# Two layers of a network on one core: the long-lived tiles 2080 bytes apart instead of 2048, the parts of the weights 4128 instead of 4096

## The chip, the cores and the metric

The kernel runs on one core of one Trainium2 chip. The metric is the device time of one execution in microseconds. Three runs of the kernel before took 2134.65, 2132.99 and 2131.47 us; the median is 2132.99 us. A core has five instruction streams: TensorE (PE; its weight loads are listed apart as PEld), VectorE (DVE), ScalarE (ACT), GpSimd (POOL) and SyncE (SP, which here issues DMAs). They run beside each other and meet at semaphores.

## What is computed

The input is one sequence of 512 tokens with 1024 features, and everything is float32. Three blocks follow one another.

1. A mixed block: RMS norm, one wide projection `h @ w_in`, sparse attention over 8 heads (a compressed branch, a selected branch and a window branch, gated), retention over 4 heads, two output projections gated and summed, `w_out`, then an MLP `square(relu(h @ w_up)) @ w_down` with 4096 hidden features.
2. An mLSTM layer (8 heads, a stabilised matrix memory) with a convolutional feed-forward of 2816 hidden features behind it: `h @ w_up`, a causal convolution of width 3 along the tokens, a GELU gate, `@ w_down`.
3. A forgetting-attention layer (16 heads) on keys and values that are projected once, and the same kind of feed-forward.

Most of the arithmetic is in products of 512 tokens with weight matrices of 1024 to 5632 columns:

```
h = rmsnorm(x, norm);  proj = h @ w_in;  ...;  x = x + mixer(proj) @ w_out
h = rmsnorm(x, norm);  x = x + act(h @ w_up) @ w_down
```

## The kernel before, in words

**Where tiles lie.** On-chip memory has 128 partitions, and a tile of shape [128, 512] in float32 takes 2048 bytes of each. Such a tile is called a unit here. Units come from one pool by tag: tag "u" has 48 buffers for what lives long (the activations' two halves, the residual stream, queries, keys, values, outputs of projections), "P" has 8, "PT" 12 and "e" 5 for short-lived ones (line 25). The buffers of a tag lie one behind the other, so that those of "u" start 2048 bytes apart. The function `unit` (line 210) picks tag and buffers. Raw weights land in two tiles of 8192 bytes (`raw`, line 150). Their two parts lie in four buffers `wh` and four `wl` of 1024 columns, 4096 bytes each (lines 167 and 168). As the program is laid out, every unit and every part begins at one remainder of its address modulo 512 bytes, which is 480; a slice of 128 columns is 512 bytes, so that nearly every operand of a large product begins there too. This remainder is called the phase below.

**How a product is made.** Float32 precision comes from three products of rounded operands. A weight block is split by ScalarE into a rounded part `wh` (line 169) and by VectorE, for a few chunks by GpSimd, into the rest `wl = raw - wh` (line 171). An activation tile is split in the same way into `hi` and `lo` (`split`, from line 369). Then `mm3` (lines 474 to 478) multiplies `hi` by `wh`, `lo` by `wh` and `hi` by `wl` into one accumulator. The weight is the stationary operand, 128 columns at a time, and the activation streams by with 512 columns, or 256 where a product is cut into halves of the tokens. In `gemm_tok` (from line 569) the parts are exchanged: 128 tokens of the activation are stationary, and 272, 280, 384 or 512 columns of the weight stream by.

Where a weight block has 280 or 272 columns, one `wh` buffer holds two rows of blocks behind each other, so that the second row starts 1120 or 1088 bytes into the buffer. The second chunk of such a raw block starts 2240 or 2176 bytes into `raw`, while its parts start at the beginning of their buffers.

**Order.** SyncE loads weight block i+2 while block i+1 is split and block i is multiplied (`Weights.get`). Beside the large products, a generator of attention work (`fill`, `tick`) puts small matmuls between the large ones in the mixed, mLSTM and attention stages. The feed-forward stages have large products only. Before the two feed-forwards of the second network the residual tiles are written to DRAM by GpSimd's queue and read back by SyncE's.

Of the kernel before, what the change touches and what calls it, by code (L numbers as in the profile page):

```python
# [9 lines left out]
F32 = mybir.dt.float32  # L10
# [14 lines left out]
BUFS = {"u": 48, "P": 8, "PT": 12, "e": 5}  # L25
# [89 lines left out]
class Weights:  # L115
# [40 lines left out]
    def split_steps(self, i):  # L156

        kt, cols, _ = self.plan[i]
        raw, v = self.raw[i]
        kk = self.CH // cols  # L160
        if kk == 3:
            kk = 2
        res = self.parts[i] = []
        for k0 in range(0, kt, kk):
            n = min(kk, kt - k0)
            a, b = k0 * cols, (k0 + n) * cols
            h = self.pp.tile([128, self.CH], F32, tag="wh", name="wh")
            l = self.pp.tile([128, self.CH], F32, tag="wl", name="wl")
            self.nc.scalar.activation(h[:, 0:b - a].bitcast(F32R), raw[:, a:b], AF.Copy)  # L169
            e = self.nc.gpsimd if (i, k0 // kk) in self.pool else self.nc.vector  # L170
            e.tensor_tensor(l[:, 0:b - a].bitcast(F32R), raw[:, a:b], h[:, 0:b - a], op=OP.subtract)  # L171
            for k in range(n):
                res.append(tuple(t[:, k * cols:(k + 1) * cols].bitcast(F32R) for t in (h, l)))
            yield
# [20 lines left out]
def block_kernel(ctx: ExitStack, tc: tile.TileContext, I, out):  # L195
# [4 lines left out]
    up = ctx.enter_context(tc.tile_pool(name="up", bufs=1))  # L200
    sm = ctx.enter_context(tc.tile_pool(name="sm", bufs=12))
    wr = ctx.enter_context(tc.tile_pool(name="wr", bufs=2))
    wh = ctx.enter_context(tc.tile_pool(name="wh", bufs=4))
# [5 lines left out]

    def unit(name="u", tag=None, dt=F32):  # L210
        tag = tag or TAGS.get(name, "u")
        return up.tile([128, 512], dt, tag=tag, name=name, bufs=BUFS[tag])

    def R(t):
        return t.bitcast(F32R)
# [1 line left out]
    def small(w, name="s"):  # L217
        return sm.tile([128, w], F32, tag=f"s{w}", name=name, bufs=12 if w <= 8 else 2)
# [83 lines left out]


    xin = [[unit(f"xi{i}{j}", "PT") for j in range(2)] for i in range(4)]
    vec0 = unit("vec0", "P")
    for j in range(2):
        for i in range(4):
            nc.sync.dma_start(xin[i][j], I["x"][0, i * 128:(i + 1) * 128, j * 512:(j + 1) * 512])
        if j == 0:
            nc.sync.dma_start(vec0[0:8, 0:128], I["norm_mix"].rearrange("l (k p) -> (l k) p", p=128))  # L310
        WT._dma(j)
    posi = unit("posi", dt=I32)
    nc.sync.dma_start(posi, I["positions"][0].partition_broadcast(128))
    cc = cst.tile([128, 4], F32, name="cc")
# [36 lines left out]
    for l in range(2):  # L351
        w = I["ffn_conv_w_2"][l].rearrange("j (n p) -> (j n) p", p=128)
# [287 lines left out]
    with in_order(tc):  # L640
# [10 lines left out]
        u = small(4, "u4")  # L651
# [446 lines left out]
    for b in range(4):  # L1098
        w = WT.get()
# [442 lines left out]
    with in_order(tc, (mybir.EngineType.Pool,)):  # L1542
        h = post_norm(Lazy(8, hsm), "norm_mix_post_2", 0, ("norm_ffn_pre_2", 0))
# [114 lines left out]
    with in_order(tc, (mybir.EngineType.Pool,)):  # L1658
        h = post_norm(Lazy(8, fox), "norm_mix_post_2", 1, ("norm_ffn_pre_2", 1))
# [63 lines left out]
```

## Time and profile before

| | |
|---|---|
| median of three runs | 2132.99 us |
| lowest and highest run | 2131.47 and 2134.65 us |
| the profiled execution's own time | 2136.78 us |
| its span, from the first to the last instruction | 2135.1 us |
| around the span | 1.68 us |
| mean granted clock of TensorE, as a share of full speed | 0.987 |
| TensorE's matmuls, busy | 2083.1 us, 10,378 instructions |
| VectorE, ScalarE, GpSimd, busy | 1190.5, 945.3 and 351.4 us |

The busy time of an engine is what its instructions cover. For matmuls the ends are modelled, because they are pipelined; two of them overlap in the table, and the distance from one start to the next is what one costs. A group of instructions is named by its line, its engine, its operation and its tiles, output first. The granted clock is 1.00 at 2.4 GHz and 0.50 at 1.2 GHz.

### The profile page before, as it was taken

The numbers are of one execution on the slowest core, as the hardware profiler recorded it, in microseconds if no ns is written. First come the engines' busy times: TensorE is split into PE (matmuls) and PEld (weight loads), VectorE is DVE, ScalarE is ACT, GpSimd is POOL, SyncE is SP. The second block draws the span as 40 slices with busy tenths as digits, with TensorE's granted clock in tenths as the row PEclk, the third lists the DMA queues.
The fourth block names the chain that finished last, engine by engine and source line by source line (L and its number), as shares of the span: only waits on it lengthen the run. The fifth ranks groups of instructions, "written<-read, shape, count | busy, mean of one in ns | idle before, by whom it ended". The sixth has DMA issues, their size and how long they took to land.

```text
span 2135.1 us, 26621 instructions
## 1 busy us (share of the span) xinstructions
PE 2083.1 (98%) x10378; PEld 1723.1 (81%) x10378; DVE 1190.5 (56%) x2023; ACT 945.3 (44%) x1622; POOL 351.4 (16%) x371
## 2 busy tenths in 40 slices
PE   8899999999999999999999999999999999999998
PEld 6667778887888888987888888889977788888887
DVE  7845446545333334767687665246465558766422
ACT  5556533344313323565454443224476535444322
POOL 5422100003101201221211110021032022111000
PEclk9899999999999999999999999999999999999999
DMA  6321112422233332432423332232422242333222
GB/s 162 109 80 41 60 60 72 134 91 81 97 99 99 99 99 79 131 94 74 123 75 99 100 98 94 89 95 78 160 76 75 63 125 80 99 99 99 89 78 71
DMA packets 242031, 198.75 MB, mean 93 GB/s; under 512 B 15183, under 2 KB 232987, under 8 KB 241905
## 3 DMA queue, kind: packets, MB, share of 16 engines
q1 hardware_dynamic: 237808, 186.11, 29.1%
q0 software_dynamic: 4096, 10.94, 1.6%
q8 instruction: 81, 1.33, 0.3%
q14 instruction: 46, 0.37, 0.1%
HBM read 190.69 MB, written 6.34 MB: 92 GB/s over the span
## 4 chain that ended last, share of the span: by engine, by line
PE 87%; DVE 7%; ACT 2%; issue 2%; POOL 1%; DMA 1%; SPq 0%; DVEq 0%; POOLq 0%; ACTq 0%
PE g L476 24%; PE g L477 24%; PE g L478 24%; PE t L876 2%; PE g L582 1%; PE g L583 1%; PE g L584 1%; DVE wl L171 1%; PE s L857 1%; PE o L1633 1%; PE o L951 1%; PE s L858 1%; DVE x L1435 1%; PE t L1320 1%; ACT wh L169 0%
## 5 line engine op out<-in xcount | busy, mean ns | idle before, releaser
L476 PE MATMUL g<-hi,wh 128*128 128x512 f32 (+1 forms) x2604 | 996.5, 383 | 6.2 <-DVE gates L749 5.5
L477 PE MATMUL g<-lo,wh 128*128 128x512 f32 (+1 forms) x2604 | 986.4, 379 | 6.0 <-DVE lo L1440 6.0
L478 PE MATMUL g<-hi,wl 128*128 128x512 f32 (+1 forms) x2604 | 986.3, 379 | 3.6 <-POOL wl L171 1.9
L171 DVE TENSOR_TENSOR wl<-raw,wh 128x1024 fp32r<-128x1024 f32 (+4 forms) x337 | 408.8, 1215 | 381.6 <-ACT wh L169 376.9
L476 PEld LDWEIGHTS g<-hi,wh 128*128 128x128 f32 x2604 | 494.3, 190 | 105.3 <-issue 13.7
L169 ACT ACTIVATE wh<-raw 128x1024 fp32r<-128x1024 f32 (+3 forms) x348 | 356.0, 1025 | 495.4 <-PE g L477 425.3
L478 PEld LDWEIGHTS g<-hi,wl 128*128 128x128 f32 x2604 | 495.2, 190 | 93.0 <-DVE wl L171 3.1
L477 PEld LDWEIGHTS g<-lo,wh 128*128 128x128 f32 x2604 | 495.5, 190 | 92.4 <-DVE lo L1440 7.2
L865 ACT ACTIVATE P<-P,mx 128x128 f32<-128x128 f32 (+3 forms) x128 | 71.5, 559 | 45.1 <-DVE mx L863 43.2
L582 PE MATMUL g<-wh,hi 128*128 128x384 f32 (+3 forms) x256 | 85.4, 333 | 0.2 <-DVE t L698 0.2
L584 PE MATMUL g<-wl,hi 128*128 128x384 f32 (+3 forms) x256 | 83.7, 327 | 0.0
L583 PE MATMUL g<-wh,lo 128*128 128x384 f32 (+3 forms) x256 | 83.6, 327 | 0.0
L1153 POOL TENSOR_TENSOR relu<-relu 128x512 f32<-128x512 f32 x32 | 40.9, 1283 | 203.8 <-ACT relu L1152 198.7
L879 ACT COPY PT<-t 128x512 f32<-128x512 f32 (+1 forms) x96 | 48.5, 505 | 30.3 <-PE t L876 29.7
L374 DVE TENSOR_TENSOR lo<-relu,hi 128x512 fp32r<-128x512 f32 x32 | 22.6, 717 | 68.9 <-ACT hi L373 68.9
L1399 POOL TENSOR_TENSOR sq<-sq 128x512 f32<-128x512 f32 x16 | 27.1, 1696 | 204.5 <-ACT sq L1393 204.0
L876 PE MATMUL t<-ident,P 128*128 128x128 f32 x320 | 53.6, 278 | 1.7 <-ACT PT L879 1.3
L863 DVE CUSTOM_DVE_ANT_0 P<-s,cdiag 128x128 f32<-128x128 f32 (+1 forms) x64 | 30.6, 489 | 43.9 <-PE s L858 39.2
L454 POOL TENSOR_TENSOR sq<-sq 128x512 f32<-128x512 f32 x12 | 18.1, 1512 | 203.9 <-ACT sq L450 199.2
L582 PEld LDWEIGHTS g<-wh,hi 128*128 128x128 f32 x256 | 48.2, 188 | 4.0 <-issue 2.2
L876 PEld LDWEIGHTS t<-ident,P 128*128 128x128 f32 x320 | 38.2, 141 | 15.6 <-ACT PT L879 7.9
L863 DVE CUSTOM_DVE_ANT_0 P<-s,cb 128x128 f32<-128x128 f32 (+1 forms) x64 | 30.4, 488 | 35.2 <-PE s L860 26.3
(934 smaller groups left out, 2193.3 us busy)
## 6 DMA issues: line engine op xcount, KB each, us to landing
raw<-in_ffn_w_up_dram SPq DMA_DIRECT2D x88, 512.0 KB, 5.2
raw<-in_w_in_dram SPq DMA_DIRECT2D x16, 1024.0 KB, 5.1
raw<-in_w_up_dram SPq DMA_DIRECT2D x16, 1024.0 KB, 5.5
raw<-in_w_down_dram SPq DMA_DIRECT2D x16, 1024.0 KB, 5.0
raw<-in_ffn_w_down_dram SPq DMA_DIRECT2D x12, 1024.0 KB, 5.0
raw<-in_mlstm_w_in_dram SPq DMA_DIRECT2D x8, 1024.0 KB, 5.3
raw<-in_fox_w_qg_dram SPq DMA_DIRECT2D x8, 1024.0 KB, 5.3
raw<-in_ffn_w_down_dram SPq DMA_DIRECT2D x6, 768.0 KB, 4.3
```

What stands on the lines that cost most here:

```text
L169: self.nc.scalar.activation(h[:, 0:b - a].bitcast(F32R), raw[:, a:b], AF.Copy)
L171: e.tensor_tensor(l[:, 0:b - a].bitcast(F32R), raw[:, a:b], h[:, 0:b - a], op=OP.subtract)
L476: T.matmul(ps, lhsT=h, rhs=R(ah), start=first, stop=False)
L477: T.matmul(ps, lhsT=h, rhs=R(al), start=False, stop=False)
L478: T.matmul(ps, lhsT=l, rhs=R(ah), start=False, stop=last)
L582: T.matmul(ps[i][:, 0:cols], lhsT=R(ah)[:, ts], rhs=h, start=first, stop=False)
L583: T.matmul(ps[i][:, 0:cols], lhsT=R(al)[:, ts], rhs=h, start=False, stop=False)
L584: T.matmul(ps[i][:, 0:cols], lhsT=R(ah)[:, ts], rhs=l, start=False, stop=last)
L863: V.tensor_tensor_reduce(out=pr[:, 0:L], in0=ps[:, 0:L], in1=cdiag[:, 512 - L:512] if cb is None else cb[:, 0:L], scale=1.0, scalar=3e38, ...
L865: A.activation(pr[:, 0:L], pr[:, 0:L], AF.Exp, scale=-1.0, bias=mx, accum_out=rs[:, i, g:g + 1])
L876: T.transpose(pt[:, c + (i - j) * 128:c + (i - j + 1) * 128], P[i][:, j * 128:(j + 1) * 128], ident)
L879: A.copy(t[:, 0:c], pt[:, 0:c])
```

## The change

Every unit with tag "u" is allocated with 520 columns and used by its first 512, so that 48 buffers start 2080 bytes apart. The parts of the weights are allocated with 1032 columns and used by their first 1024, so that eight buffers start 4128 bytes apart. The other tags and `raw` keep their sizes; what lies behind the first pool begins 1536 bytes later, which is three times 512. The 48 units and the eight parts then begin at phases 32 bytes apart from one to the next. Together they take 1792 bytes more of each partition. The diff adds and removes no instruction.

```diff
--- before
+++ after
@@ -164,8 +164,8 @@
         for k0 in range(0, kt, kk):
             n = min(kk, kt - k0)
             a, b = k0 * cols, (k0 + n) * cols
-            h = self.pp.tile([128, self.CH], F32, tag="wh", name="wh")
-            l = self.pp.tile([128, self.CH], F32, tag="wl", name="wl")
+            h = self.pp.tile([128, self.CH + 8], F32, tag="wh", name="wh")[:, 0:self.CH]
+            l = self.pp.tile([128, self.CH + 8], F32, tag="wl", name="wl")[:, 0:self.CH]
             self.nc.scalar.activation(h[:, 0:b - a].bitcast(F32R), raw[:, a:b], AF.Copy)
             e = self.nc.gpsimd if (i, k0 // kk) in self.pool else self.nc.vector
             e.tensor_tensor(l[:, 0:b - a].bitcast(F32R), raw[:, a:b], h[:, 0:b - a], op=OP.subtract)
@@ -209,7 +209,8 @@
 
     def unit(name="u", tag=None, dt=F32):
         tag = tag or TAGS.get(name, "u")
-        return up.tile([128, 512], dt, tag=tag, name=name, bufs=BUFS[tag])
+        w = 520 if tag == "u" else 512
+        return up.tile([128, w], dt, tag=tag, name=name, bufs=BUFS[tag])[:, 0:512]
 
     def R(t):
         return t.bitcast(F32R)
```

## Rows read from the trace of the kernel before

**Rows 1.** The page: span, busy engines, granted clock, shares of the chain, one group.

```profile
span 2135.1 us, 26621 instructions
...
PE 2083.1 (98%) x10378; PEld 1723.1 (81%) x10378; DVE 1190.5 (56%) x2023; ACT 945.3 (44%) x1622; POOL 351.4 (16%) x371
...
PEclk9899999999999999999999999999999999999999
...
PE 87%; DVE 7%; ACT 2%; issue 2%; POOL 1%; DMA 1%; SPq 0%; DVEq 0%; POOLq 0%; ACTq 0%
PE g L476 24%; PE g L477 24%; PE g L478 24%; PE t L876 2%; PE g L582 1%; PE g L583 1%; PE g L584 1%; DVE wl L171 1%; PE s L857 1%; PE o L1633 1%; PE o L951 1%; PE s L858 1%; DVE x L1435 1%; PE t L1320 1%; ACT wh L169 0%
...
L582 PE MATMUL g<-wh,hi 128*128 128x384 f32 (+3 forms) x256 | 85.4, 333 | 0.2 <-DVE t L698 0.2
```

**Rows 2.** Groups by line and shape: count, busy us, mean ns, idle before.

```profile
L476 PE MATMUL g<-hi,wh 128*128 128x512 f32 x2260 | 897.3, 397 | 6.2 <-DVE gates L749 5.5 <-ACT wh L169 0.8
...
L476 PE MATMUL g<-hi,wh 128*128 128x256 f32 x344 | 99.2, 292 | 0.0
```

**Rows 3.** Timeline of TensorE in a feed-forward stage: start us, us, instruction.

```profile
1229.93 0.39 PE L476 MATMUL g<-hi,wh 128*128 128x512 f32 x1
1230.15 0.39 PE L477 MATMUL g<-lo,wh 128*128 128x512 f32 x1
1230.38 0.39 PE L478 MATMUL g<-hi,wl 128*128 128x512 f32 x1
...
1232.65 0.39 PE L476 MATMUL g<-hi,wh 128*128 128x512 f32 x1
```

**Rows 4.** Windows of feed-forward stages: each engine's busy us and instructions, clock, DMA.

```profile
550.00:600.00 50.00, 50.00 (x223) 41.42 (x222) 17.98 (x19) 15.35 (x19) 6.87 (x5) 1.00 0.27 88
...
1200.00:1250.00 50.00, 50.00 (x222) 41.43 (x221) 34.42 (x43) 22.44 (x28) 5.69 (x5) 1.00 0.33 88
```

**Rows 5.** Timeline of TensorE, weights streaming 280 columns wide, then 272.

```profile
43.15 0.29 PE L582 MATMUL g<-wh,hi 128*128 128x280 f32 x1
...
44.70 0.29 PE L582 MATMUL g<-wh,hi 128*128 128x280 f32 x1
...
46.23 0.29 PE L582 MATMUL g<-wh,hi 128*128 128x280 f32 x1
...
860.94 0.29 PE L582 MATMUL g<-wh,hi 128*128 128x272 f32 x1
...
862.45 0.29 PE L582 MATMUL g<-wh,hi 128*128 128x272 f32 x1
...
863.97 0.29 PE L582 MATMUL g<-wh,hi 128*128 128x272 f32 x1
```

**Rows 6.** Timeline of VectorE: the two chunks of a weight block of 280 columns.

```profile
41.65 0.73 DVE L171 TENSOR_TENSOR wl<-raw,wh 128x560 fp32r<-128x560 f32 x1
...
42.64 0.73 DVE L171 TENSOR_TENSOR wl<-raw,wh 128x560 fp32r<-128x560 f32 x1
```

**Rows 7.** Timeline of TensorE where attention matmuls stand between the large ones.

```profile
1612.20 0.40 PE L477 MATMUL g<-lo,wh 128*128 128x512 f32 x1
1612.44 0.40 PE L478 MATMUL g<-hi,wl 128*128 128x512 f32 x1
1612.67 0.40 PE L476 MATMUL g<-hi,wh 128*128 128x512 f32 x1
1612.90 0.39 PE L477 MATMUL g<-lo,wh 128*128 128x512 f32 x1
1613.13 0.39 PE L478 MATMUL g<-hi,wl 128*128 128x512 f32 x1
1613.36 0.28 PE L857 MATMUL s<-ks,qs 128*128 128x256 f32 x1
```

**Rows 8.** Windows of the three mixed stages, of instructions on the large products' accumulators.

```profile
50.00:300.00 250.00, 159.98 (x617) 110.04 (x616) 18.00 (x36) 14.18 (x26) 0.95 0.23 70
850.00:1080.00 230.00, 188.48 (x949) 157.30 (x948) 14.67 (x26) 13.06 (x26) 0.98 0.34 106
1420.00:1760.00 340.00, 261.07 (x1348) 215.12 (x1347) 21.15 (x36) 14.21 (x32) 0.98 0.31 94
```

**Rows 9.** Waits for a DMA: us in total, times, longest us.

```profile
POOL nMd L1294 <- DMA nM<-dM: 18.1, 6, 4.3
ACT wh L169 <- DMA raw<-in_w_in_dram: 10.6, 3, 4.5
```

## Prediction

> **What bounds the kernel now.** I read the page first. TensorE is busy 98% of the span and carries 87% of the chain of waits; VectorE has 7% of it, ScalarE 2%, DMA 1%, and the granted clock stands at nine tenths or more in every slice [rows 1]. So the question is what one matmul costs, how much of that depends on addresses, and whether the few ends of VectorE and ScalarE on the chain depend on them.
>
> Next come the groups by shape. 2,260 matmuls of 512 columns and 344 of 256 stand on line 476, and as many on 477 and on 478; the token products add 768 on lines 582 to 584, three times 256 [rows 1, 2]. Together these are 8,580, of which 6,780 have 512 columns. Their listed mean of 397 ns is no cost, since ends are modelled; starts are what counts. In a feed-forward stage the twelve starts from 1229.93 to 1232.65 us lie 2.72 us apart, 226.7 ns each [rows 3]. At 2.4 GHz 512 columns stream in 213.3 ns, so each matmul has 13.3 ns that are not streaming. 6,780 times 226.7 ns is 1,537 us, 72% of the span.
>
> **The change part by part.** Nothing is removed, added or moved: the same instructions in the same order on every queue, the same waits, the same DMA sizes. What changes is where operands begin. Of a large product the streaming operand (a unit of tag "u") and the stationary one (a part of the weights) begin at one phase now and would differ by any multiple of 32 bytes afterwards. Units of tag "P" and "PT" and `raw` keep their phase. The change can act in four places.
>
> *Engines hindering one another on the memory.* If equal phases made TensorE wait for ScalarE or VectorE, a matmul would take longer where those are busy. Between 1200 and 1250 us VectorE is busy 34.4 us of 50 and ScalarE 22.4; between 550 and 600 it is 18.0 and 15.4. TensorE has 222 matmuls in the first and 223 in the second [rows 4], in step with 226.7 ns (50 us over that is 220.6, and those that reach over the edges count too). Twice the traffic costs not one matmul. The gain to be had here is 0, and the loss too, since phases in these windows are as equal as they can be.
>
> *Stationary against streaming operand.* This is the disputed price: the 13.3 ns could be the two reads of TensorE meeting at equal phase. The bounds are a gain of all of it and a loss. The nearest rows are matmuls whose two operands already differ in phase: the second row of blocks in a buffer begins 1120 bytes (280 columns) or 1088 bytes (272 columns) in, 96 or 64 bytes away from the stationary operand's phase; the first row begins at equal phase. At 280 columns twelve matmuls of the second row take 1.55 us (43.15 to 44.70) and twelve of the next first row 1.53 (44.70 to 46.23). At 272 the first row takes 1.51 us (860.94 to 862.45) and the second 1.52 (862.45 to 863.97) [rows 5]. By streaming plus 13.3 ns they would take 1.56 and 1.52. So a shift of phase takes nothing away; it comes with 0.01 to 0.02 us more for twelve, 0.8 to 1.7 ns for one, and the rows are rounded to 0.01 us. I take 0 for the term, and keep both ends: minus 13.3 ns and plus 1.7 ns.
>
> The Trainium skill says of back-to-back matmuls ("TensorE: Matmul & The Clock Gate", the section "Wait — 56ns, not 53.3ns?") that a start-to-start distance is N over 2.4 GHz plus about 2.5 ns once warm, 215.7 ns at 512 columns. The rows have 226.7 ns, 11 ns more, so the page leaves room for something in this kernel that costs 11 ns a matmul; if that were the phase, 8,580 times 11 ns, an estimate of 94 us from that page, would go. The rows at other phases do not bear that out, since they keep their distance.
>
> *ScalarE and VectorE.* The split of a weight chunk reads `raw` and the part. In a block of 280 columns the first chunk has `raw` and `wl` at one phase, the second begins 2240 bytes into `raw`, 192 bytes away in phase: both take 0.73 us [rows 6]. That is equal to 0.01 us, 1.4%. Line 171 has 1% of the chain, 21 us [rows 1]; 1.4% of that is 0.3 us at most, either way. The rest of VectorE's share, 6% or 128 us, is small operations and evacuations that read one unit and an accumulator bank; by the same 1.4% 1.8 us is the bound, and I take 0.
>
> *DMAs.* Residual tiles are written out and read back in rows of 2048 bytes, from and to units whose phases change. Only two waits for a DMA show at all, 18.1 us for `nM`, a unit of "PT", and 10.6 us for the first weights [rows 9]. Neither tile changes size, and `raw` moves by 1536 bytes, a multiple of 512. The cover of the residual tiles is the product that runs meanwhile; without it the cost would show as a new wait in this view, and one of the size of the longest there would be 4.5 us.
>
> The sum for the profiled execution is 2136.78 + 0 us. That execution lies 3.8 us above the median of the runs, 2132.99, and its span is 1.68 us shorter than its time. For the median of the runs the forecast is 2133.0 us.
>
> **The rivals.** *Faster, all of it.* If most differences of phase, other than 64 and 96 bytes, freed TensorE's two reads, 8,580 times 13.3 ns, 114 us, would go: 2019 us. For it speaks that the 13.3 ns stand everywhere at equal phase; against it, rows 5. A tenth of it would be 2122 us. Chance 3%. By the rule of the Trainium skill's page on TensorE, cited above, the same rival would give back an estimated 94 us, 2039 us, with no chance beyond these 3%.
>
> *Faster, in the mixed stages.* Where attention work stands between the large matmuls, starts lie further apart: 1612.20 to 1613.36 us holds five distances of 232 ns, 5.3 ns more than in the feed-forward [rows 7]. Units of all sorts are read and written there by all engines, and spreading them could help. The three mixed stages have 617, 949 and 1,348 matmuls on the large accumulators, 2,914 [rows 8]; by 5.3 ns that is 15 us as a ceiling (2118), and if one in two is affected and half of that is phase, 4 us (2129). Against it: the feed-forward has as much traffic at the same phases without any excess [rows 4], so the excess goes with the mix of instructions. Chance of more than 4.3 us: 8%.
>
> *Slower: a streaming operand off the common phase costs TensorE a little.* The place is every large matmul whose unit has moved; the price is the 0.8 to 1.7 ns of rows 5, which have the sign of a loss both times. It decides when the price is above 0.5 ns, since 8,580 times 0.5 ns is 4.3 us. At 0.8 ns it gives 6.9 us (2140), at 1.7 ns 14.6 us (2147.6). Against it: by streaming plus 13.3 ns the shifted rows are no slower than they ought to be, it is the unshifted ones that are a little quick, and a rounding of 0.01 us covers half of it. Chance 10%.
>
> *The change does not do what it says*, because the spacing is rounded back to something that keeps equal phases or because nothing reads the phase. It gives 2133 too and is part of the forecast. Ends of stages that shift by some nanoseconds can change which stretches get the lower clock; that is in the spread.
>
> **How the numbers follow.** 0.2% of the median is 4.3 us, about what a measurement of this kernel can tell from no change. The forecast, within that, has 77%; its own range is 2129 to 2137 us, the spread of the three runs (3.2 us) plus the 1.8 us of VectorE and the 0.3 us of the split. The faster rivals have 3% and 8%, the slower one 10%, and a DMA that comes late, 4.5 us, 2%. That makes faster 11%, same 77%, slower 12%. The range for 8 in 10 reaches to 2126 below, half of the mixed stages' ceiling, and to 2142 above, the slower rival at 1.0 ns.
>
> **What would show it.** After the change, starts in a feed-forward stage should lie 226.7 ns apart again, 2.72 us for twelve; 2.59 us would be the first rival in full, 2.73 or more the slower one. The two chunks of a 280-column block should take 0.73 us still. In the mixed stages five distances around 232 ns should remain. The chain should keep TensorE at 87%, and no wait for a residual tile's DMA should appear. The prediction is wrong if the median moves by more than 4.3 us, and its reasoning is wrong, whatever the time, if a steady distance differs from 226.7 ns by over 0.5 ns.

## The result: 1.25% slower

The changed kernel took 2159.1 us in the median of four runs (2158.26 to 2160.56), the kernel before 2132.2 us in the runs beside them (2129.75 to 2134.65). The ratio is 1.0125, 95% interval 1.0113 to 1.0138: 26.9 us slower, where no change was forecast and 2142 us was the end of the range. The profiled execution took 2158.62 us, with a span of 2156.9 us.

The page of the changed kernel, the lines that answer to [rows 1]:

```profile
span 2156.9 us, 26621 instructions
...
PE 2102.6 (97%) x10378; PEld 1715.4 (80%) x10378; DVE 1191.8 (55%) x2023; ACT 946.0 (44%) x1622; POOL 351.9 (16%) x371
...
PE 89%; DVE 6%; ACT 2%; issue 1%; DMA 1%; POOL 0%; SPq 0%; DVEq 0%; POOLq 0%; ACTq 0%
PE g L477 25%; PE g L478 24%; PE g L479 24%; PE g L583 2%; PE g L584 2%; PE g L585 2%; PE t L877 2%; DVE wl L171 1%; PE s L858 1%; PE o L952 1%; PE o L1634 1%; PE s L859 1%; DVE x L1436 1%; PE t L1321 0%; DVE qs L387 0%
```

Every engine has the same number of instructions, and VectorE, ScalarE and GpSimd are as busy as before to within 1.3 us. Only TensorE's share of the chain grew, from 87% to 89%. The place is its steady stream. The timeline of TensorE in the same feed-forward stage, against [rows 3]:

```profile
1239.92 0.40 PE L477 MATMUL g<-hi,wh 128*128 128x512 f32 x1
1240.15 0.39 PE L478 MATMUL g<-lo,wh 128*128 128x512 f32 x1
...
1242.24 0.39 PE L478 MATMUL g<-lo,wh 128*128 128x512 f32 x1
1242.47 0.39 PE L479 MATMUL g<-hi,wl 128*128 128x512 f32 x1
```

Eleven distances take 2.55 us, 231.8 ns each instead of 226.7. The windows of the feed-forward stages, against [rows 4] (each engine's busy us and instructions, then clock, DMA share, GB/s), say it once more: 217 matmuls in 50 us instead of 223 and 222, at full clock, with the other engines about as busy.

```profile
550.00:600.00 50.00, 50.00 (x217) 40.53 (x217) 18.08 (x20) 16.51 (x21) 6.86 (x5) 1.00 0.26 85
1200.00:1250.00 50.00, 50.00 (x217) 40.51 (x217) 33.69 (x42) 22.08 (x27) 5.19 (x4) 1.00 0.32 86
```

Now let each matmul stand for the time from its start to the next start. Summed over the trace, those of lines 476 to 478 (477 to 479 after) with 512 columns take 1593.6 us before and 1622.8 after, 29.2 us more, or 4.3 ns each. Those with 256 columns take 141.0 and 137.6. The profiled execution before spent more time at the lower clock (granted clock 0.987 against 0.992), so the two profiled executions lie only 21.8 us apart where the medians lie 26.9 apart. Of the 3.4 us at 256 columns about half is no more than clock: at full clock, neighbouring large matmuls of 256 columns start 119.9 ns apart before and 118.3 after, which is 1.7 us over 1,032 of them. A kernel that appears further down, with parts 256 bytes wider, kept the old distances and ran at 0.992 too. Against its trace (1594.0 and 137.8 us, span 2128.7) the changed kernel takes 28.8 us more at 512 columns, 0.2 less at 256, and 28.2 more in the whole span. So the loss is the 512-column matmuls, within 1 us.

### The profile page after: what moved, and what is told of

It is laid out like the page before. It is cut to its first block, busy times and chain, and to the rows that moved or that the text cites. A ratio compares the mean times of both kernels' runs of the same rounds, so it can differ in the third digit from the quotient of the medians.

```text
span 2156.9 us, 26621 instructions
## 1 busy us (share of the span) xinstructions
PE 2102.6 (97%) x10378; PEld 1715.4 (80%) x10378; DVE 1191.8 (55%) x2023; ACT 946.0 (44%) x1622; POOL 351.9 (16%) x371
## 3 DMA queue, kind: packets, MB, share of 16 engines
q1 hardware_dynamic: 237808, 186.11, 28.8%
## 4 chain that ended last, share of the span: by engine, by line
PE 89%; DVE 6%; ACT 2%; issue 1%; DMA 1%; POOL 0%; SPq 0%; DVEq 0%; POOLq 0%; ACTq 0%
PE g L477 25%; PE g L478 24%; PE g L479 24%; PE g L583 2%; PE g L584 2%; PE g L585 2%; PE t L877 2%; DVE wl L171 1%; PE s L858 1%; PE o L952 1%; PE o L1634 1%; PE s L859 1%; DVE x L1436 1%; PE t L1321 0%; DVE qs L387 0%
## 5 line engine op out<-in xcount | busy, mean ns | idle before, releaser
L375 DVE TENSOR_TENSOR lo<-relu,hi 128x512 fp32r<-128x512 f32 x32 | 21.8, 691 | 70.3 <-ACT hi L374 70.3
```

## The experiments

Three theories were set against each other. Pair theory: a matmul pays for the difference in phase between its own two operands. Step theory: it pays where a phase differs from that of the matmul before. Traffic theory: other engines' accesses at new phases disturb TensorE.

### One half of the change alone, and one constant shift

Units only: the diff's second hunk without its first.

```diff
+        w = 520 if tag == "u" else 512
-        return up.tile([128, 512], dt, tag=tag, name=name, bufs=BUFS[tag])
+        return up.tile([128, w], dt, tag=tag, name=name, bufs=BUFS[tag])[:, 0:512]
```

> Only the units of tag u are 2080 bytes apart; the parts of the weights stay 4096 apart. The whole change took 2159.1 us against 2132.2. Pair theory (each matmul pays for the phase between its own two operands): nearly the whole loss, 2150 to 2160 us, since every unit has its own phase against parts of one phase. Step theory (a matmul pays when a phase differs from that of the matmul before it): also most of the loss, 2150 to 2160, since hi and lo alternate. Traffic theory (VectorE and ScalarE writing parts at new phases disturb TensorE): little, below 2140, since the parts have not moved.

2151.7 us, ratio 1.0086 (1.0071 to 1.0101): 19 us slower, at the low end of what two theories expected. Traffic theory as it was put there falls, since the parts had not moved. The activations had, and the other engines write those too; that wider form falls with the first probe below.

Parts only: the first hunk without the second.

```diff
-            h = self.pp.tile([128, self.CH], F32, tag="wh", name="wh")
+            h = self.pp.tile([128, self.CH + 8], F32, tag="wh", name="wh")[:, 0:self.CH]
```

(and the same for `l`)

> Only the parts of the weights are 4128 bytes apart; the units stay 2048 apart. Pair theory: a loss too, 2140 to 2160 us, since each of the eight buffers stands at a phase of its own. Step theory: smaller, 2135 to 2148, since the stationary phase changes in two of three matmuls but the streaming one never does. Traffic theory: the whole loss, 2150 to 2160.

2160.1 us, ratio 1.0129 (1.0112 to 1.0146): the whole loss. The parts alone cost as much as both halves and the units alone 71% of that, so the halves do not add. Step theory expected 2148 at most. Pair theory explains why they do not add: once the differences are spread over all phases, spreading them twice changes nothing; and with units alone, the activations in "P" and "PT" buffers still meet the parts at equal phase. The trace of units alone bears this out. From 389 to 426 us, where the two output projections stream tiles of those tags, the starts lie as close as before:

```profile
395.84 0.39 PE L477 MATMUL g<-hi,wh 128*128 128x512 f32 x1
...
398.56 0.39 PE L477 MATMUL g<-hi,wh 128*128 128x512 f32 x1
```

Twelve distances take 2.72 us, 226.7 ns each. Of 216 steady stretches of 24 large matmuls in this trace, 25 have a mean under 227.5 ns; in the traces of the whole change and of the parts alone no stretch has.

A constant shift: the spacings of before, and a padding tile between the pools.

```diff
+    gap = ctx.enter_context(tc.tile_pool(name="gap", bufs=1))
+    gap_t = gap.tile([128, 64], F32, name="gap_t")
+    nc.vector.memset(gap_t, 0.0)
```

> The spacings are those of before; 256 bytes of padding stand between the pools, so that every part of the weights lies half of 512 bytes away in phase from every unit, by one constant difference. Pair theory: all large matmuls change alike, so the time differs from before clearly, either way, by 10 us or more (per matmul a constant between -10 and +10 ns). Step theory: no change, 2132 us within 4.3. Traffic theory: no change.

2133.3 us, ratio 1.0000 (0.9991 to 1.0009). Taken alone this speaks for step theory and against pair theory with its phases modulo 512. The first probe settled it the other way.

### The price by itself

The first probe's inner loop, cut out of the kernel; all operands lie in two tiles, `st` (stationary) and `mv` (streaming), of one phase. F32R is float32r, the type by which the large products of the kernel read their rounded operands:

```python
        e = 8 * i
        for j in range(NB):
            m = {"A": e, "B": e * (j % 2), "C": 0, "D": e}[kind]
            s = 128 * (j % 4) + (e * (j % 2) if kind == "C" else 0)
            T.matmul(ps[:, 0:n], lhsT=st[:, s:s + 128].bitcast(F32R), rhs=mv[:, m:m + n].bitcast(F32R),
                     start=(j == 0), stop=(j == NB - 1))
```

> Computes none of the reference: 54 blocks of 33 matmuls in the form of the large ones (float32r, 128 stationary columns from four slices 512 bytes apart, 512 streaming columns, 256 in the last 8 blocks), with the other engines idle. Blocks A: streaming operand 32 i bytes off the stationary one's phase, i = 0 to 15, constant within a block. Blocks B: the streaming operand alternates between two addresses 32 i bytes apart. Blocks C: the stationary one does. Blocks D: as A, with 256 columns and every second i. Pair theory: the start-to-start distance in A depends on i, between 226 and 237 ns, and in B and C it is the mean of two values of A. Step theory: A is 226.7 ns for all i, B and C are longer by 2 to 10 ns for some i. Traffic theory: 226.7 ns in all blocks, since nothing else runs.

The timeline of TensorE, one row for each block of 33 matmuls: the difference of two starts, divided by 33, is the distance. Blocks Ab to Aj are i = 1 to 9 at 512 columns, Da to Dk i = 0, 2, 4, 6, 8, 10 at 256; Aa, i = 0, ran partly at the lower clock and is left out.

```profile
17.46 7.86 PE L62 MATMUL blkAb<-mv,st 128*128 128x512 f32 x33
25.16 7.73 PE L62 MATMUL blkAc<-mv,st 128*128 128x512 f32 x33
32.73 7.87 PE L62 MATMUL blkAd<-mv,st 128*128 128x512 f32 x33
40.44 7.86 PE L62 MATMUL blkAe<-mv,st 128*128 128x512 f32 x33
48.14 7.89 PE L62 MATMUL blkAf<-mv,st 128*128 128x512 f32 x33
55.87 7.86 PE L62 MATMUL blkAg<-mv,st 128*128 128x512 f32 x33
63.57 7.86 PE L62 MATMUL blkAh<-mv,st 128*128 128x512 f32 x33
71.27 7.65 PE L62 MATMUL blkAi<-mv,st 128*128 128x512 f32 x33
78.75 7.86 PE L62 MATMUL blkAj<-mv,st 128*128 128x512 f32 x33
...
361.12 4.12 PE L62 MATMUL blkDa<-mv,st 128*128 128x256 f32 x33
365.07 4.05 PE L62 MATMUL blkDc<-mv,st 128*128 128x256 f32 x33
368.96 4.08 PE L62 MATMUL blkDe<-mv,st 128*128 128x256 f32 x33
372.88 3.94 PE L62 MATMUL blkDg<-mv,st 128*128 128x256 f32 x33
376.65 4.10 PE L62 MATMUL blkDi<-mv,st 128*128 128x256 f32 x33
380.59 4.05 PE L62 MATMUL blkDk<-mv,st 128*128 128x256 f32 x33
```

Within a block A or D no phase steps, and no other engine works beyond copying one column at a block's end. Yet Ab takes 233.3 ns (25.16 less 17.46, over 33), Ac 229.4, Ad to Ah 233 to 234, and Ai, with 256 bytes, 226.7. From there it repeats: Aj is Ab again, and so on to i = 15. So the period is 256 bytes, and the shift by 256 was a shift by nothing. Step and traffic theories fall as the whole cause. At 256 columns the order is another: 119.7 ns at 0, 117.9 at 64 bytes, 118.8 at 128, 114.2 at 192, 119.4 at 256. With the start of each block left out, the values at 512 columns are 226.7 (i = 0, by Ai), 233.3, 228.9, 233.3, 233.3, 234.4, 233.3 and 233.3 ns. If the means of such values added up simply, a kernel with all differences alike in number would show their mean, 232.1, and the changed kernel showed 231.8.

Blocks B and C contradict the pair theory in its simplest form: only about half of them are the mean of two values of A. Streaming addresses that alternate 192 bytes apart (Bg) gave 226.7 ns where the mean is 230. Nor does the period hold throughout there: stationary addresses that alternate 32 bytes apart (Cb) gave 230.0 ns, and 256 bytes more (Cj) 235.1. What came before has a part in it, which was not taken further.

There is a second thing that these probes cannot tell. The trace of before shows that the weights of one matmul are loaded while the matmul ahead of it streams: the load for line 478 begins with the matmul of line 477, which starts at 1230.15 us [rows 3].

```profile
1230.16 0.19 PEld L478 LDWEIGHTS g<-hi,wl 128*128 128x128 f32 x1
```

So what counts may be a streaming operand and its own stationary one, as pair theory says, or a streaming operand and the next matmul's stationary one. In blocks A all stationary slices have one phase, and both readings give the same times.

### The period in the whole kernel

> The spacings are those of before; 128 bytes of padding stand between the pools, so that every part of the weights differs from every unit by 128 bytes modulo 256, by one constant. In the first probe a constant difference of 128 bytes gave 233.3 ns against 226.7 at 512 columns and 118.6 against 120.0 at 256. Pair theory, with a period of 256 bytes: 6,780 times 6.7 ns less 1,032 times 1.4 ns, 44 us more, 2170 to 2178 us, worse than the whole change. Step theory: 2132 us, no change. Traffic theory: 2132 us.

The padding tile of above with 32 columns instead of 64. 2164.1 us, ratio 1.0152 (1.0135 to 1.0169): no spacing is changed, and the kernel is slower than the one in question. The sign is as pair theory expects it, the size, 31 us, is under the 44. Against the trace with parts 256 bytes wider (the next run), the matmuls of 512 columns take 32.0 us more, 4.7 ns each instead of the 6.7 of the probe, and those of 256 columns 0.3 us less. In steady stretches they start 232.4 ns apart, 5.7 ns more, which is nearer; the rest of the difference to the probe was not explained.

> Only the parts of the weights are spaced wider, as in the kernel with 4128 bytes that took 2160 us, but by 256 bytes, 4352 apart. Pair theory with a period of 256 bytes: no change, 2132 us within 4. Any theory in which the wider spacing itself costs (the slices, the allocation, other banks): 2145 to 2160 us.

The same line as in the parts alone, with `self.CH + 64`. 2131.1 us, ratio 0.9995 (0.9985 to 1.0004): no change. Wider parts cost 28 us at 32 bytes more and nothing at 256. The windows 550:600 of four kernels, in the order parts alone, 256 bytes wider, shifted by 128, units alone:

```profile
550.00:600.00 50.00, 50.00 (x217) 40.60 (x216) 16.77 (x18) 17.06 (x21) 7.61 (x6) 1.00 0.26 85
```

```profile
550.00:600.00 50.00, 50.00 (x223) 41.39 (x222) 18.01 (x19) 15.15 (x19) 6.87 (x5) 1.00 0.32 106
```

```profile
550.00:600.00 50.00, 50.00 (x217) 40.55 (x216) 18.07 (x20) 16.41 (x20) 6.87 (x5) 1.00 0.26 85
```

```profile
550.00:600.00 50.00, 50.00 (x219) 40.85 (x218) 16.99 (x18) 15.71 (x20) 6.87 (x5) 1.00 0.30 96
```

The counts of TensorE's matmuls are 217 where the phases differ, 223 where they are equal, and 219 where a part of the activations kept its place.

> Computes none of the reference: 192 blocks of 21 matmuls as in blocks A of the first probe, with the streaming operand 0, 4, 8 ... 252 bytes off the stationary one's phase, at 512 columns (blocks W), 256 (blocks H) and 384 (blocks T). Pair theory: the multiples of 32 bytes repeat the first probe at 512 columns (226.7, 233.3, 228.9, 233.3, 233.3, 234.4, 233.3, 233.3 ns) and at 256 columns every second of them (120.0, 117.8, 118.6, 113.3); what lies between them nobody has measured, and a value below 226.7 ns at 512 columns would make a faster kernel. Step and traffic theories: one distance for all blocks of a width.

The timeline of TensorE, blocks of 21 matmuls: 512 columns at 108 bytes (Wdd) and 120 (Wdg), 256 columns at equal phase (Haa) and at 16 bytes (Hae).

```profile
140.87 4.93 PE L57 MATMUL blkWdd<-mv,st 128*128 128x512 f32 x21
145.63 5.01 PE L57 MATMUL blkWde<-mv,st 128*128 128x512 f32 x21
...
155.46 5.20 PE L57 MATMUL blkWdg<-mv,st 128*128 128x512 f32 x21
160.49 5.01 PE L57 MATMUL blkWdh<-mv,st 128*128 128x512 f32 x21
...
322.35 2.67 PE L57 MATMUL blkHaa<-mv,st 128*128 128x256 f32 x21
324.86 2.74 PE L57 MATMUL blkHab<-mv,st 128*128 128x256 f32 x21
...
332.54 2.54 PE L57 MATMUL blkHae<-mv,st 128*128 128x256 f32 x21
334.92 1.26 PE L57 MATMUL blkHaf<-mv,st 128*128 128x256 f32 x9
```

Over a whole block Wdd takes 226.7 ns a matmul, Wdg 239.5, Haa 119.5 and Hae 113.3. The following values are those of the last 12 distances of each block. All of blocks W lie between 226.7 and 240.0 ns: none of the 64 differences is faster than equal phase, so at 512 columns the kernel before has a layout that no other in this grid beats. Five differences, 28, 60, 108, 156 and 252 bytes, are as good. Blocks H lie between 113.3 and 126.6 ns, with 120.0 at equal phase; blocks T between 173.3 and 180.6, with 173.3 there.

### A layout that takes what is left

> The kernel before, with the parts of the weights 4352 bytes apart (which changed nothing) and, for the weight blocks that are multiplied with 256 columns alone, begun 64 bytes later in their buffer, so that the streaming operand lies 192 bytes ahead modulo 256. The probes gave 113.3 ns there against 120.0 at equal phase. Pair theory: 1,032 matmuls times 6.7 ns, 6.9 us less, 2125 to 2128 us, all other matmuls as before. If only a steady row of identical pairs gains, or other work sets the pace where the halves run: 2132 us.

```diff
+            o = 16 if i in self.halved else 0
-            h = self.pp.tile([128, self.CH], F32, tag="wh", name="wh")
+            h = self.pp.tile([128, self.CH + 64], F32, tag="wh", name="wh")[:, o:o + self.CH]
```

(and the same for `l`; `halved` holds the weight blocks that `gemm(halves=True)` and `gemm_halves` use, and the lines that fill it are left out here)

2128.2 us against 2133.4, ratio 0.9984 (0.9974 to 0.9994): 5.2 us faster in the medians, of the 6.9 expected. The timeline of TensorE where 256 columns stream, in the kernel before and in this one:

```profile
1086.00 0.28 PE L478 MATMUL g<-hi,wl 128*128 128x256 f32 x1
...
1089.24 0.28 PE L478 MATMUL g<-hi,wl 128*128 128x256 f32 x1
```

```profile
1080.03 0.28 PE L489 MATMUL g<-hi,wl 128*128 128x256 f32 x1
...
1083.09 0.28 PE L489 MATMUL g<-hi,wl 128*128 128x256 f32 x1
```

The same 27 distances take 3.24 us before, 120.0 ns each, and 3.06 here, 113.3 ns each. Over all neighbouring large matmuls of 256 columns at full clock the means are 119.9 and 114.3 ns; for 1,032 that is 5.7 us, close to the 5.2 measured. This beats both kernels, by little.

### Which operands, and why the rows misled

> Computes none of the reference: 32 blocks of 33 matmuls with 512 streaming columns, the streaming operand 32 i bytes off the stationary one's phase, i = 0 to 7. Blocks S: float32r with one and the same stationary slice; blocks N: both operands bfloat16; blocks F: both plain float32; blocks X: float32r, the streaming operand 2048 bytes further than in the first probe. Pair theory: X repeats 226.7, 233.3, 228.9, 233.3, 233.3, 234.4, 233.3, 233.3 ns; S depends on i too, by about as much; for N and F nothing is known, and if what counts is bytes of the two operands that meet, N, with half the bytes, gains or loses less than 7 ns over i. Step and traffic theories: one distance within each kind.

The timeline of TensorE, two starts of each form: bfloat16 (N), plain float32 (F, two records for one matmul).

```profile
79.98 7.29 PE L73 MATMUL blkNb<-mb,sw 128*128 128x512 bf16 x33
87.11 7.29 PE L73 MATMUL blkNc<-mb,sw 128*128 128x512 bf16 x33
...
158.16 28.49 PE L73 MATMUL blkFb<-mv,st 128*128 128x512 f32 x66
186.49 28.49 PE L73 MATMUL blkFc<-mv,st 128*128 128x512 f32 x66
```

All eight blocks N run at 215.8 ns and all eight blocks F at 858.3 ns a matmul; the phase does nothing there. X repeats A, and S, with one stationary slice, is the same as A too.

The 215.8 ns lie within 0.1 ns of the 215.7 that the Trainium skill gives for 512 columns ("TensorE: Matmul & The Clock Gate", "Wait — 56ns, not 53.3ns?"). So its rule holds for bfloat16 here, and the 11 ns above it in this kernel come with float32r even at its best phase. The page "SBUF — State Buffer" of the Trainium skill ("Who interferes with whom") lists TensorE's two reads, of the streaming operand and of the weights, as independent. The blocks in bfloat16 and plain float32 agree with that; for float32r the distance depends on where the two operands lie to each other, by up to 13 ns in blocks W.

> Computes none of the reference: 24 blocks of 33 float32r matmuls, the streaming operand 32 i bytes off the stationary one's phase, i = 0 to 7. Blocks Q: 512 columns in the order of the kernel, with two streaming tiles 4096 bytes apart and two stationary ones. Blocks Y: 272 columns. Blocks Z: 280 columns. Pair theory: Q as in the first probe, 226.7 at i = 0 and 228 to 235 elsewhere; at i = 4 nearer to the 232.4 ns that the kernel with 128 bytes of padding showed than to 233.3 if the order of the operands matters. If the rows at 272 and 280 columns misled the prediction because the price depends on the width, Y and Z differ by under 2 ns between i = 0 and i = 2 and 3, while Q differs by 2 to 7 ns; if not, Y and Z cost as Q does.

The timeline of TensorE, blocks at 272 columns (Y) and 280 (Z), a for equal phase, c for 64 bytes, d for 96:

```profile
72.40 4.30 PE L58 MATMUL blkYa<-mv,st 128*128 128x272 f32 x33
76.54 4.31 PE L58 MATMUL blkYb<-mv,st 128*128 128x272 f32 x33
80.69 4.34 PE L58 MATMUL blkYc<-mv,st 128*128 128x272 f32 x33
84.87 4.34 PE L58 MATMUL blkYd<-mv,st 128*128 128x272 f32 x33
...
105.58 4.38 PE L58 MATMUL blkZa<-mv,st 128*128 128x280 f32 x33
109.80 4.38 PE L58 MATMUL blkZb<-mv,st 128*128 128x280 f32 x33
...
118.20 4.41 PE L58 MATMUL blkZd<-mv,st 128*128 128x280 f32 x33
122.44 4.42 PE L58 MATMUL blkZe<-mv,st 128*128 128x280 f32 x33
```

At 272 columns 125.5 ns at equal phase and 126.7 at 64 bytes; at 280 columns 127.9 and 128.5 at 96. [Rows 5] held 125.8 and 126.7, and 127.5 and 129.2, within 1 ns of these and with the same sign: the rows were read rightly. They were too few to give a size, though. Unrounded, six pairs of rows at 272 columns in the trace of before differ by 0.2 to 0.7 ns a matmul, all with this sign; at 280 columns the pair shown differs by 1.2 ns and the next pair by nothing. At 512 columns the same 64 bytes cost 2.2 ns and the same 96 bytes 6.7. Block Q at 128 bytes took 233.3 ns, as in A, so the order of the operands is not why the kernel shifted by 128 showed 232.4.

## Why the prediction was wrong, point by point

- **The failed step is "Stationary against streaming operand".** Its term was taken as 0, with plus 1.7 ns as the far end. It measured 5.1 ns a matmul at 512 columns in a feed-forward stage, three times the end, and 4.3 ns as a mean over all 6,780, from one trace to the other. The rows behind it were matmuls of 272 and 280 columns, and the last probe shows that the price of a phase depends on the width: 1.2 and 0.6 ns there, 2.2 and 6.7 at 512, and a gain of up to 6.7 at 256. The prediction carried a price from one shape to another without naming that as an assumption.
- **The reading of the 13.3 ns was half right.** They are no price of equal phase; none of 64 differences is cheaper at 512 columns. But the prediction took "no gain from other phases" for "no dependence".
- **The slower rival named the place and the sign**, every large matmul whose unit has moved, and its price was too low. It had 10%. Both pairs of rows had the sign of a loss, and the rounding of 0.01 us was used to wave them away. The rounding did hide the size, which at these widths is a nanosecond or less; but with 8,580 matmuls a nanosecond is 8.6 us, so rows that cannot tell a nanosecond could not bring the chance of a loss down to 10%.
- **The range** ended at 2142 us by the same rows. An operation whose phase no row shows at its own width has no bound from above; the honest end was open.
- **Engines hindering one another: right.** The probe has the same prices with the other engines idle, and the windows after are no different under more or less traffic.
- **ScalarE and VectorE: right.** Line 171 at 560 columns takes 0.73 us twice in the changed kernel as in [rows 6]:

```profile
42.27 0.73 DVE L171 TENSOR_TENSOR wl<-raw,wh 128x560 fp32r<-128x560 f32 x1
...
43.26 0.73 DVE L171 TENSOR_TENSOR wl<-raw,wh 128x560 fp32r<-128x560 f32 x1
```

- **DMAs: right as to the residual tiles**, for which no wait appears. A wait of VectorE for `cb` shows instead, 8.5 us in four times, a "PT" unit whose size did not change; whether it costs anything on the chain was not tried:

```profile
DVE P L864 <- DMA cb<-dC: 8.5, 4, 4.1
```

- **The faster rivals** fell as to the time: no phase gives the 13.3 ns back at 512 columns. In the halves of the tokens spreading did help, 1.6 ns a matmul at full clock and 1.7 us in all, which the prediction had not priced. The five distances of [rows 7], which were to stay around 232 ns, take 1.15 us in the changed kernel (1628.23 to 1629.38), 230 ns each: at that place nothing was lost, and nothing to speak of gained.
- **The two tests of the prediction's last part worked**: a steady distance off by more than 0.5 ns was named as the sign that the reasoning is wrong, and it is the first thing that the trace shows.
- **Slips without weight.** The granted clock is not nine tenths in every slice: the second digit in [rows 1] is an 8. The token products hold 96 more matmuls of 512 columns, so these are 6,876 in all. By the prediction's own 13.3 ns its first rival in full would show twelve distances of 2.56 us, not 2.59.

What is shown is that the loss comes with the address difference between the streaming and the stationary operands of float32r matmuls: constant differences reproduce it with the other engines idle, and spacings of 256 bytes take it away. What stays open is the mechanism within the chip, whether a matmul's own stationary operand counts or that of the next, why float32r alone of the three types depends on the phase, the part that the matmul before plays, and the 0.9 ns by which the kernel shifted by 128 bytes was quicker than its probe.

## What to carry to other kernels

In a kernel bound by float32r matmuls with 512 streaming columns, let the streaming and the stationary operand begin at one address modulo 256 bytes: a spacing wider by 256 bytes cost nothing, and 32 bytes of well-meant padding cost 1.25% here. A price per instruction that is multiplied by thousands has to come from rows of the very same shape, or from a probe; a neighbouring width has another price. And a control should be checked against the period that it might share with the effect: the first constant shift here was a whole period, and by itself would have pointed to the wrong theory.

## What the runs showed of the hardware that was not expected

- For float32r the start-to-start distance depends on the difference between the two operands' addresses, with a period of 256 bytes: 226.7 to 240.0 ns at 512 columns, 173.3 to 180.6 at 384, 113.3 to 126.6 at 256, over 64 differences in steps of 4 bytes. The period held wherever the difference stayed constant; where the stationary address alternated, 32 bytes and 288 bytes gave 230.0 and 235.1 ns.
- None of the 64 differences is better than equal phase at 512 columns, and several are at 256, where 16, 112 and 192 bytes gave 113.3 ns against 120.0.
- bfloat16 (215.8 ns) and plain float32 (858.3 ns) at 512 columns showed no dependence at eight phases.
